# Projecting keys, queries and values for attention with 512 moving columns instead of 256

## The chip, the cores and the metric

The kernel runs on one core of one Trainium2 chip. The metric is the device time of one execution in microseconds (us), as the median of several runs. The profile and the trace are of one further execution. TensorE is PE in the profile (PEld: its weight loads), VectorE DVE, ScalarE ACT, GpSimd POOL, SyncE SP.

## The reference

512 tokens of 1024 channels go through two layers. Layer A is a state-space mixer with a gated feed-forward block; layer B is attention with a gated feed-forward block. What matters here is the attention of layer B: keys and values are projected from the normed stream, queries from the layer's own normed stream, keys and queries get an RMS norm per head, and the attention is stick-breaking.

```python
def shared_kv(h, kv_norm, w_kv, k_norm):
    k, v = jnp.split(rms_norm(h, kv_norm) @ w_kv, 2, axis=-1)
    k = rms_norm(k.reshape(bsz, seq, N_HEADS, HEAD_DIM), k_norm)
    v = v.reshape(bsz, seq, N_HEADS, HEAD_DIM)

def stick_breaking_attention(q, k, v):
    # A[t,s] = beta_ts * prod_{s<j<t}(1 - beta_tj), s < t
    z = jnp.einsum('bqhd,bkhd->bhqk', q, k) * HEAD_DIM ** -0.5
    log_beta = jax.nn.log_sigmoid(z)
    log_1m = jnp.where(causal, log_beta - z, 0.0)
    later = lax.cumsum(log_1m, axis=3, reverse=True) - log_1m
    w = jnp.where(causal, jnp.exp(log_beta + later), 0.0)
    return jnp.einsum('bhqk,bkhd->bqhd', w, v)

def sb_mixer(xn, w_q, q_norm, k, v, w_o):
    q = rms_norm((xn @ w_q).reshape(bsz, seq, N_HEADS, HEAD_DIM), q_norm)
    return stick_breaking_attention(q, k, v).reshape(bsz, seq, D_MODEL) @ w_o
```

There are 16 heads of 64 channels; all values are float32.

## The kernel before

Every large product is three matmuls: both operands are split into a rounded high half (fp32r) and the rest, and high by high, high by low and low by high are added in PSUM. `WStream` brings the weights in pieces: a DMA on SP loads a piece into one of three raw buffers (`_load`), ACT writes the high half (`high`, L116 or, with a gain, L119), DVE the low half (`low`, L130 or L133), each into one of `OUT` = 3 buffers. `take()` hands out the next piece and prepares `look` = 2 pieces ahead.

The attention stage runs from 601 to 862 us of the span. Its **main work** is the projection. `project(g)` for g = 0 to 3 takes four heads, and for each in turn keys, queries and values: 256 output columns over 4 token blocks and 8 blocks of channels. The token block of the stream is the stationary operand, the weight half the moving one, with 256 columns (L458 to L460). Two PSUM banks hold the four token blocks; after g = 0, which runs alone and uses banks 0 to 5, all projections use banks 0 and 1. Then values are copied out by ACT with the row scale (L465). Keys and queries are copied to `raw` (L470, two buffers), squared by ACT (L472), summed per head by DVE (L475), turned into a factor by some sixteen tiny DVE operations (L476 to L481, with `rsqrt` at L200 to L207), multiplied by it (L484, DVE), queries also by the gain row `grow` on POOL (L487), and split into a high half (L490, ACT) and a low half (L491, DVE): the tiles `ks` and `qs`, one buffer each.

The **side work** is the attention of the eight pairs of heads. `steps(pair)` does for each pair: transposes of `ks` and `qs` on PE (L517), copies of the result (L521; L525 to L527 for `kpad`), scores (`z`, L536, banks 2 to 4), two sigmoids on ACT (L558, L559), a scan and a product on DVE (L565, L566), transposes of the weights (L584, banks 5 and 7), a copy on ACT (L588), the product with values (L597, bank 6) and the copy of the output (L618, or straight into its halves). The scores of a pair lie in five units of up to 512 columns, so there are 40 units in the stage.

`schedule()` deals the side work out in small steps by the list `PAIR`. `attention()` issues one step of the projection after another and as many side steps as `MAIN_RATIO` allows; what is left of the side work goes between the matmuls of the output projection (`wo_part`, L250 to L252, by `WO_RATIO`), whose input is the pairs' outputs and whose result DVE adds to the stream (L657). After this a scheduler reorders each engine's instructions within what the buffers allow; the program's final order is therefore not the written one.

## Time and profile before

| | |
|---|---|
| median of 3 runs | 1239.07 us (1238.36 to 1240.52) |
| profiled execution, its own time | 1241.04 us |
| its span in the trace | 1239.3 us |
| PE busy in the span | 1199.9 us (97%) |
| DVE busy | 776.4 us (63%) |
| ACT busy | 542.9 us (44%) |
| POOL busy | 143.0 us (12%) |
| attention stage | about 601 to 862 us of the span |

The busy time of an engine is the sum of its instructions' times, where overlapping ones count once. Matmuls are pipelined: the duration of one (0.28 us with 256 columns) is longer than the distance from its start to the next one's start, and it is this distance that the time of a run of matmuls is made of. An engine's idle time costs something only where the others wait for it.

### The profile page before, as it was taken

The numbers are of one execution on the slowest core, as the hardware profiler recorded it, in microseconds if no ns is written. First come the engines' busy times: TensorE is split into PE (matmuls) and PEld (weight loads), VectorE is DVE, ScalarE is ACT, GpSimd is POOL, SyncE is SP. The second block draws the span as 40 slices with busy tenths as digits, with TensorE's granted clock in tenths as the row PEclk, the third lists the DMA queues.
The fourth block names the chain that finished last, engine by engine and source line by source line (L and its number), as shares of the span: only waits on it lengthen the run. The fifth ranks groups of instructions, "written<-read, shape, count | busy, mean of one in ns | idle before, by whom it ended". The sixth has DMA issues, their size and how long they took to land. (4 is left out here: it accounts for less than half of the span.)

```text
span 1239.3 us, 17202 instructions
## 1 busy us (share of the span) xinstructions
PE 1199.9 (97%) x6831; PEld 1012.5 (82%) x6831; DVE 776.4 (63%) x1246; ACT 542.9 (44%) x869; POOL 143.0 (12%) x132
## 2 busy tenths in 40 slices
PE   7888899999999999999999999999999999999998
PEld 7777777888888888888999898776788888888887
DVE  7969545867565564333579998976775556552322
ACT  7644543444333333222358676645453433332210
POOL 4878720000000000000000000000300000000000
PEclk8889999999999999999999999999999999999999
DMA  7333232333333333333321121121333333322330
GB/s 191 107 85 90 74 103 85 103 87 101 102 91 96 102 91 92 103 96 96 103 86 58 63 69 52 52 69 35 95 92 97 91 95 92 102 102 88 125 111 34
DMA packets 162379, 111.68 MB, mean 90 GB/s; under 512 B 7452, under 2 KB 151868, under 8 KB 162236
## 3 DMA queue, kind: packets, MB, share of 16 engines
q1 hardware_dynamic: 161724, 109.55, 29.9%
q8 instruction: 53, 0.87, 0.3%
q10 hardware_dynamic: 576, 1.05, 0.2%
q14 instruction: 26, 0.21, 0.1%
HBM read 101.93 MB, written 2.10 MB: 84 GB/s over the span
## 5 line engine op out<-in xcount | busy, mean ns | idle before, releaser
L250 PE MATMUL b<-t_xhi,t_whi 128*128 128x512 f32 x864 | 336.6, 392 | 2.6 <-ACT p_w L1340 1.4
L251 PE MATMUL b<-t_xlo,t_whi 128*128 128x512 f32 x864 | 337.3, 391 | 1.4 <-DVE t_xlo L168 0.8
L252 PE MATMUL b<-t_xhi,t_wlo 128*128 128x512 f32 x864 | 336.9, 390 | 0.2 <-DVE t_wlo L130 0.2
L116 ACT CAST t_whi<-t_wraw 128x1024 fp32r<-128x1024 f32 (+1 forms) x166 | 173.1, 1044 | 361.0 <-PE b L251 240.6
L130 DVE TENSOR_TENSOR t_wlo<-t_wraw,t_whi 128x1024 fp32r<-128x1024 f32 (+1 forms) x154 | 189.2, 1230 | 151.4 <-ACT t_whi L116 150.5
L250 PEld LDWEIGHTS b<-t_xhi,t_whi 128*128 128x128 f32 x864 | 162.4, 188 | 38.1 <-ACT p_w L1340 1.9
L251 PEld LDWEIGHTS b<-t_xlo,t_whi 128*128 128x128 f32 x864 | 162.4, 188 | 36.8 <-DVE t_xlo L168 2.7
L252 PEld LDWEIGHTS b<-t_xhi,t_wlo 128*128 128x128 f32 x864 | 162.3, 188 | 34.6 <-DVE t_wlo L130 0.6
L458 PE MATMUL b<-t_whi,t_xhi 128*128 128x256 f32 x384 | 109.3, 286 | 1.4 <-ACT a_raw L470 1.3
L460 PE MATMUL b<-t_whi,t_xlo 128*128 128x256 f32 x384 | 109.1, 285 | 0.0
L459 PE MATMUL b<-t_wlo,t_xhi 128*128 128x256 f32 x384 | 109.1, 285 | 0.0
L315 DVE TENSOR_TENSOR p_fg<-b,p_rsrow 128x512 f32<-128x512 f32 x44 | 30.4, 691 | 86.9 <-PE b L252 80.5
L458 PEld LDWEIGHTS b<-t_whi,t_xhi 128*128 128x128 f32 x384 | 73.2, 191 | 1.9 <-ACT a_raw L470 1.8
L326 DVE TENSOR_TENSOR p_fv<-b,p_rsrow 128x512 f32<-128x512 f32 x44 | 30.4, 690 | 69.5 <-PE b L252 69.5
L459 PEld LDWEIGHTS b<-t_wlo,t_xhi 128*128 128x128 f32 x384 | 73.4, 191 | 0.2
L460 PEld LDWEIGHTS b<-t_whi,t_xlo 128*128 128x128 f32 x384 | 73.2, 191 | 0.2
L250 PE MATMUL b<-p_ahi,t_whi 128*128 128x512 f32 x176 | 68.5, 389 | 0.0
L251 PE MATMUL b<-p_alo,t_whi 128*128 128x512 f32 x176 | 68.5, 389 | 0.0
L252 PE MATMUL b<-p_ahi,t_wlo 128*128 128x512 f32 x176 | 68.5, 389 | 0.0
L348 PE MATMUL b<-t_whi,p_ahi 128*128 128x512 f32 x176 | 68.5, 389 | 0.0
L349 PE MATMUL b<-t_wlo,p_ahi 128*128 128x512 f32 x176 | 68.5, 389 | 0.0
L350 PE MATMUL b<-t_whi,p_alo 128*128 128x512 f32 x176 | 68.5, 389 | 0.0
(307 smaller groups left out, 1892.9 us busy)
## 6 DMA issues: line engine op xcount, KB each, us to landing
t_wraw<-in_ffn_w_up_dram SPq DMA_DIRECT2D x88, 512.0 KB
t_wraw<-in_ffn_w_down_dram SPq DMA_DIRECT2D x30, 512.0 KB
t_wraw<-in_a_w_glu_dram SPq DMA_DIRECT2D x16, 512.0 KB
t_wraw<-in_w_kv_dram SPq DMA_DIRECT2D x16, 512.0 KB
t_wraw<-in_ffn_w_down_dram SPq DMA_DIRECT2D x16, 448.0 KB
t_wraw<-in_a_w_in_dram SPq DMA_DIRECT2D x8, 512.0 KB
p_w<-p_w2d SPq DMA_DIRECT2D x32, 128.0 KB
t_wraw<-in_b_w_q_dram SPq DMA_DIRECT2D x8, 512.0 KB
```

The lines of the kernel that those rows point to most:

```text
L116: nc.scalar.copy(hi, t)
L130: eng.tensor_tensor(out=lo, in0=t, in1=hi, op=ALU.subtract)
L250: nc.tensor.matmul(ps, whi, xhi, start=start, stop=False)
L251: nc.tensor.matmul(ps, whi, xlo, start=False, stop=False)
L252: nc.tensor.matmul(ps, wlo, xhi, start=False, stop=stop)
L315: nc.vector.tensor_tensor(out=g, in0=pg, in1=rr, op=ALU.mult)
L348: nc.tensor.matmul(pss[tb], xh, whi[:, j], start=k + j == 0, stop=False)
L349: nc.tensor.matmul(pss[tb], xh, wlo[:, j], start=False, stop=False)
L350: nc.tensor.matmul(pss[tb], xl, whi[:, j], start=False, stop=st)
L458: nc.tensor.matmul(reg[tb], xh, whi[:, j], start=st, stop=False, skip_group_check=True)
L459: nc.tensor.matmul(reg[tb], xh, wlo[:, j], start=False, stop=False, skip_group_check=True)
L460: nc.tensor.matmul(reg[tb], xl, whi[:, j], start=False, stop=k == 7, skip_group_check=True)
```

## The change

The projection is cut into six phases, `kq0, v0, kq1, kq2, v1, kq3`. A `kq` phase makes keys and queries of four heads, side by side as 512 columns; a `v` phase makes values of eight heads, also 512 columns. In a phase the four token blocks come one after the other, each with 24 matmuls of 512 columns (L501 to L503 now) into one bank, 0 and 1 in turn. All four pieces of the weights of a phase (two channel blocks by 512 columns each) have to be there for that, so there are five high and low buffers instead of three, two of them in the attention's pool (`half_tile`), and `AHEAD` prepares the next phase's pieces during the present one. A piece of a `kq` phase comes in two DMAs.

Keys and queries share one norm per phase: four norms with 32 factors instead of eight with 16. Each token block's bank is copied to `raw` by ACT (L509), squared in place in PSUM by ACT (L510) and summed by DVE out of PSUM (L511). `raw` has one buffer instead of two, the product with the factors is written back into it (L535), and `kh` is gone. The side work runs by `MAIN_RATIO` 0.85 after a delay of eight main steps; there are six instead of seven tiles for the attention weights. To make room, one row tile (`grow1`) moves from the constants into the pool of the first layer's setup, so that its load and the two POOL operations that use it come later.

```diff
     def _load(self, i):
         ap, nk, nc_, gain = self.plan[i][:4]
         t = self.e.tile([P, nk, nc_], F32, "wraw", self.RAW)
-        self.e.nc.sync.dma_start(t, ap.rearrange("(k p) c -> p k c", p=P))
+        for c, (a, _) in self.parts(i):
+            self.e.nc.sync.dma_start(t[:, :, c], a.rearrange("(k p) c -> p k c", p=P))
         self.raw[i] = t
+
+    def parts(self, i):
+
+        ap, nk, nc_, gain = self.plan[i][:4]
+        if not isinstance(ap, tuple):
+            return [(slice(0, nc_), (ap, gain))]
+        n = nc_ // len(ap)
+        return [(slice(j * n, (j + 1) * n), x) for j, x in enumerate(ap)]
+
+    def half_tile(self, i, tag):
+        shape = [P, *self.plan[i][1:3]]
+        if self.room is not None and (i - self.room[1]) % (self.OUT + 2) >= self.OUT:
+            return self.room[0](shape, F32R, tag, 2)
+        return self.e.tile(shape, F32R, tag, self.OUT)
 
...
-        hi = e.tile([P, nk, nc_], F32R, "whi", self.OUT)
+        hi = self.half_tile(i, "whi")
...
-                nc.scalar.activation(hi[:, k], t[:, k], AF.Copy, scale=gain[:, k : k + 1])
+                for c, (_, g) in self.parts(i):
+                    nc.scalar.activation(hi[:, k, c], t[:, k, c], AF.Copy, scale=g[:, k : k + 1])
...
+        self.prepare(i + self.look)
+        return self.done.pop(i)
+
+    def prepare(self, m):
...
-    acc = e.pt(pool, [P, T + LINE], F32, "ssacc")[:, :T]
+    acc = e.pt(pool, [P, T + 7 * LINE], F32, "ssacc")[:, :T]
...
+PHASES = (("kq", 0), ("v", 0), ("kq", 1), ("kq", 2), ("v", 1), ("kq", 3))
+
+AHEAD = {(2, 0): 1, (3, 1): 2, (3, 2): 3, (3, 3): 4}
+
+
 def attn_plan(w_kv, w_q, gkv, gb):
     plan = []
-    for g in range(4):
-        for w, c0, gain in ((w_kv, 0, gkv), (w_q, 0, gb), (w_kv, D, gkv)):
-            for k in (0, 4):
-                plan.append((w[k * P : (k + 4) * P, c0 + g * 256 : c0 + (g + 1) * 256], 4, 256, gain[:, k : k + 4]))
+    for kind, g in PHASES:
+        for k in range(0, DC, 2):
+            rows = slice(k * P, (k + 2) * P)
+            if kind == "v":
+                src = ((w_kv[rows, D + g * T : D + (g + 1) * T], gkv[:, k : k + 2]),)
+            else:
+                c = slice(g * 256, (g + 1) * 256)
+                src = ((w_kv[rows, c], gkv[:, k : k + 2]), (w_q[rows, c], gb[:, k : k + 2]))
+            plan.append((src, 2, T, True))
...
-MAIN_RATIO = 0.792
+MAIN_RATIO = 0.85
+
+DELAY = 8
...
-WB = 7
+WB = 6
...
-RB = 2
-KB = 1
...
+    def project(self, kind, g):
+        e, nc, ws = self.e, self.nc, self.ws
+        first = ws.i
+        tiles = []
+        if kind == "v":
+            out = self.t([P, 4, T], F32, "v", 2)
+        else:
+            out = self.t([P, 4, T], F32, "raw")
+            ms = self.t([P, 4, 8], F32, "hms")
+        for tb in range(4):
+            ps = e.bank(tb % 2)
+            for piece in range(4):
+                if tb == 0:
+                    tiles.append(ws.take())
+                elif (tb, piece) in AHEAD:
+                    ws.prepare(first + 4 + AHEAD[tb, piece])
+                whi, wlo = tiles[piece]
+                for j in range(2):
+                    k = 2 * piece + j
+                    xh = self.xhi[k][:, tb * P : (tb + 1) * P]
+                    xl = self.xlo[k][:, tb * P : (tb + 1) * P]
+                    nc.tensor.matmul(ps, xh, whi[:, j], start=k == 0, stop=False)
+                    nc.tensor.matmul(ps, xh, wlo[:, j], start=False, stop=False)
+                    nc.tensor.matmul(ps, xl, whi[:, j], start=False, stop=k == 7)
+                if piece < 3:
+                    yield
+            if kind == "v":
+                nc.scalar.activation(out[:, tb], ps, AF.Copy, scale=self.r4[:, tb : tb + 1])
+            else:
+                nc.scalar.copy(out[:, tb], ps)
+                nc.scalar.activation(ps, ps, AF.Square)
+                nc.vector.tensor_reduce(
+                    out=ms[:, tb], in_=ps.rearrange("p (h d) -> p h d", d=HD), axis=mybir.AxisListType.X, op=ALU.add)
+            if tb < 3:
+                yield
+        if kind == "v":
+            for i in range(2):
+                self.v[2 * g + i] = out[:, :, 256 * i : 256 * i + 256]
+        else:
+            self.norm(g, out, ms)
+        yield
+    def norm(self, g, raw, ms):
+        e, nc = self.e, self.nc
+        S = [P, 4, 8]
+        flat = lambda t: t.rearrange("p a b -> p (a b)")
+        nc.vector.tensor_tensor(out=ms, in0=ms, in1=self.r4sq.unsqueeze(2).broadcast_to(S), op=ALU.mult)
+        nc.vector.tensor_scalar(out=ms, in0=ms, scalar1=EPS, scalar2=None, op0=ALU.add)
+        f = self.t(S, F32, "hf")
+        rsqrt(e, flat(f), flat(ms), [P, 32], "hr")
+        nc.vector.tensor_tensor(out=f, in0=f, in1=self.r4.unsqueeze(2).broadcast_to(S), op=ALU.mult)
+        for i, kind in enumerate("kq"):
+            H = [P, 4, 4, HD]
+            kh = raw[:, :, 256 * i : 256 * i + 256].rearrange("p a (b c) -> p a b c", c=HD)
+            nc.vector.tensor_tensor(
+                out=kh, in0=kh, in1=f[:, :, 4 * i : 4 * i + 4].unsqueeze(3).broadcast_to(H), op=ALU.mult)
+            if kind == "q":
+                nc.gpsimd.tensor_tensor(
+                    out=kh, in0=kh, in1=self.grow.unsqueeze(1).unsqueeze(1).broadcast_to(H), op=ALU.mult)
+            ks = self.t([P, 16, 2, HD], F32R, f"{kind}s", SB)
+            hi, lo = (ks[:, :, j].rearrange("p (a b) c -> p a b c", a=4) for j in range(2))
+            nc.scalar.copy(hi, kh)
+            nc.vector.tensor_tensor(out=lo, in0=kh, in1=hi, op=ALU.subtract)
+            self.st[g, kind] = ks
...
-        for _ in a.project(0):
+        ws.room = a.t, ws.i
+        for _ in a.project(*PHASES[0]):
             pass
         side = a.schedule()
-        n = main = 0
-        for g in range(1, 4):
-            for _ in a.project(g):
+        n, main = 0, -DELAY
+        for phase in PHASES[1:]:
+            for _ in a.project(*phase):
                 main += 1
                 while n < main * MAIN_RATIO:
                     next(side, None)
                     n += 1
+        ws.room = None
...
-        self.gr = [e.tile([P, HD], F32, f"grow{i}") for i in range(2)]
+        self.gr = [e.tile([P, HD], F32, "grow0")]
...
-            gr = self.gr
+            gr = self.gr + [e.pt(pool, [P, HD], F32, "grow1")]
             nc.sync.dma_start(gr[0], a["k_norm"].partition_broadcast(P))
             nc.sync.dma_start(gr[1], a["b_q_norm"][0].partition_broadcast(P))
             nc.gpsimd.tensor_tensor(out=gr[0], in0=gr[0], in1=gr[1], op=ALU.mult)
```

Three places show how the order of the instructions moves. The names are those of the buffers: `b_0_5390` is a use of PSUM bank 0, the last number tells uses apart; `t_xhi_5223` to `5230` are the eight channel blocks of the stream; `a_ks`, `a_qs`, `a_raw`, `a_w` are the tiles named above.

**First place**, PE, where the first block of the projection ends and a bank is used again. Before, keys of the first four heads end in bank 1, and queries go on in banks 2 and 3:

```order
L458 MATMUL b_1_5285<-t_whi,t_xhi_5227 128x256
L459 MATMUL b_1_5285<-t_wlo,t_xhi_5227 128x256
L460 MATMUL b_1_5285<-t_whi,t_xlo_5235 128x256
L458 MATMUL b_2_5437<-t_whi,t_xhi_5220 128x256
L459 MATMUL b_2_5437<-t_wlo,t_xhi_5220 128x256
L460 MATMUL b_2_5437<-t_whi,t_xlo_5228 128x256
```

Now token blocks 0 and 1 of `kq0` alternate and end within three matmuls of each other, and token block 2 goes into bank 0 at once:

```order
L501 MATMUL b_0_5289<-a_whi,t_xhi_5230 128x512
L501 MATMUL b_1_5362<-a_whi,t_xhi_5230 128x512
L502 MATMUL b_0_5289<-a_wlo,t_xhi_5230 128x512
L503 MATMUL b_0_5289<-a_whi,t_xlo_5238 128x512
L502 MATMUL b_1_5362<-a_wlo,t_xhi_5230 128x512
L503 MATMUL b_1_5362<-a_whi,t_xlo_5238 128x512
L501 MATMUL b_0_5390<-t_whi,t_xhi_5223 128x512
L502 MATMUL b_0_5390<-t_wlo,t_xhi_5223 128x512
```

The use of a free bank between two uses of bank 0 is gone here.

**Second place**, where the transposes of a new `ks` stand. PE before (third pair; `b_0` and `b_1` are banks of a projection that is under way):

```order
L459 MATMUL b_1_6632<-t_wlo,t_xhi_5226 128x256
L517 MATMUL b_5_6705<-p_identr,a_ks 128x128 x4
L597 MATMUL b_6_6449<-a_wt,a_v 64x512 x2
L517 MATMUL b_7_6713<-p_identr,a_ks 128x128 x4
L460 MATMUL b_1_6632<-t_whi,t_xlo_5234 128x256
L458 MATMUL b_0_6631<-t_whi,t_xhi_5227 128x256
```

PE now (third pair; `b_1_6137` is token block 1 of `kq2`, `b_0_6199` its token block 2):

```order
L503 MATMUL b_1_6137<-t_whi,t_xlo_5238 128x512
L648 MATMUL b_6_5838<-a_wt,a_v 64x512 x2
L568 MATMUL b_7_6059<-p_identr,a_ks 128x128 x4
L568 MATMUL b_5_6067<-p_identr,a_ks 128x128 x4
L635 MATMUL b_7_6075<-t_ident,a_w 128x128 x4
L501 MATMUL b_0_6199<-t_whi,t_xhi_5223 128x512
```

and DVE now at the same place (the norm of `kq1` ends with L535; `b_0_6084` is token block 0 of `kq2`, in the bank that `b_0_6199` wants):

```order
L535 TENSOR_TENSOR a_raw<-a_raw,a_hf 128x4x256 x2
L543 TENSOR_TENSOR a_ks<-a_raw,a_ks 128x16x64
L617 TENSOR_TENSOR a_w<-a_w,a_cp_5283 128x128
L617 TENSOR_TENSOR a_w<-a_w,a_cp_5283 128x384
L616 SCALAR_TENSOR_TENSOR a_cp_5281<-a_cp_5281,p_edge 128x256 x2
L617 TENSOR_TENSOR a_w<-a_w,a_cp_5281 128x256 x2
L669 COPY a_o_5959<-b_6_5838 128x512
L576 CAST a_kpad_5265<-b_7_6059 128x512
L543 TENSOR_TENSOR a_qs<-a_raw,a_qs 128x16x64
L576 CAST a_kpad_5267<-b_5_6067 128x512
L578 CAST a_kpad_5266<-b_7_6059 64x512
L511 TENSOR_REDUCE a_hms<-b_0_6084 128x8
```

Before, main matmuls that waited for nothing stood around the transposes; now the transposes of `ks` and a bank that has to be emptied stand one behind the other on PE.

**Third place**, PE behind the last matmul of the projections. Before, the first transposes of `ks` behind it are those of the seventh pair:

```order
L252 MATMUL b_0_7783<-t_xhi_7769,t_wlo 128x512
L517 MATMUL b_7_7738<-p_identr,a_ks 128x128 x4
L250 MATMUL b_0_7783<-t_xhi_7773,t_whi 128x512
L251 MATMUL b_0_7783<-t_xlo_7774,t_whi 128x512
L252 MATMUL b_0_7783<-t_xhi_7773,t_wlo 128x512
L597 MATMUL b_6_7492<-a_wt,a_v 64x512 x2
L517 MATMUL b_5_7746<-p_identr,a_ks 128x128 x4
```

Now they are those of the sixth:

```order
L587 MATMUL b_2_6817<-a_kpad_5267,a_fmq 128x256
L587 MATMUL b_2_6817<-a_kpad_5268,a_fmq 128x256
L568 MATMUL b_5_6829<-p_identr,a_ks 128x128 x4
L648 MATMUL b_6_6627<-a_wt,a_v 64x512 x2
L568 MATMUL b_7_6837<-p_identr,a_ks 128x128 x4
L273 MATMUL b_0_7074<-t_xhi_7070,a_whi 128x512
```

In all, 11 of the 40 units of scores stood behind the last projection matmul on PE, and 20 stand there now. Up to the last product with values, PE changed 129 times between projection or output-projection matmuls and side work, and changes 89 times now.

## Rows read from the trace of the kernel before

**Rows 1.** Windows: span, busy of PE, PEld, DVE, ACT, POOL, granted clock, DMA share, GB/s.

```profile
601.00:640.00 39.00, 39.00 (x326) 38.92 (x325) 27.58 (x82) 19.60 (x41) 4.54 (x14) 1.00 0.27 89
640.00:792.00 152.00, 150.40 (x1204) 137.97 (x1203) 138.25 (x297) 107.20 (x206) 7.78 (x4) 1.00 0.20 63
792.00:862.00 70.00, 65.12 (x348) 47.33 (x347) 51.87 (x81) 35.33 (x61) 0.00 (x0) 1.00 0.18 53
```

**Rows 2.** Timeline of PE, projection without side work: start, duration, instruction; 26 steps apart.

```profile
613.76 0.28 PE L458 MATMUL b<-t_whi,t_xhi 128*128 128x256 f32 x1
...
616.88 0.28 PE L460 MATMUL b<-t_whi,t_xlo 128*128 128x256 f32 x1
```

**Rows 3.** Timeline of PE, 512 columns in the feed-forward block; 15 steps apart.

```profile
1149.78 0.39 PE L348 MATMUL b<-t_whi,p_ahi 128*128 128x512 f32 x1
...
1153.18 0.39 PE L348 MATMUL b<-t_whi,p_ahi 128*128 128x512 f32 x1
```

**Rows 4.** Timeline of PE, side work between projection matmuls.

```profile
681.41 0.63 PE L536 MATMUL b<-a_kpad,a_fmq 128*128 128x256 f32 x4
681.98 1.08 PE L597 MATMUL b<-a_wt,a_v 128*64 128x384 f32 x8
683.00 0.66 PE L584 MATMUL b<-t_ident,a_w 128*128 128x128 f32 x4
...
683.78 0.35 PE L458 MATMUL b<-t_whi,t_xhi 128*128 128x256 f32 x1
683.97 0.28 PE L459 MATMUL b<-t_wlo,t_xhi 128*128 128x256 f32 x1
```

**Rows 5.** Timeline of PE at a wait; in brackets idle time and what ended it.

```profile
771.79 0.28 PE L460 MATMUL b<-t_whi,t_xlo 128*128 128x256 f32 x1
773.42 0.39 PE L458 MATMUL b<-t_whi,t_xhi 128*128 128x256 f32 x1 [1.35 <-ACT a_raw L470]
```

**Rows 6.** Lines by shape, 595 to 870 us: count, busy us, mean ns, idle before.

```profile
L133 DVE SCALAR_TENSOR_TENSOR t_wlo<-t_wraw,t_va,t_whi 128x256 fp32r<-128x256 f32 x92 | 44.0, 523 | 10.8 <-ACT t_whi L119 10.7
L484 DVE TENSOR_TENSOR a_kh<-a_raw,a_hf 128x1024 f32<-128x1024 f32 x8 | 9.8, 1222 | 0.2
L475 DVE TENSOR_REDUCE a_hms<-a_kh 128x16 f32<-128x1024 f32 x8 | 9.8, 1219 | 3.0 <-ACT a_kh L472 3.0
L470 ACT COPY a_raw<-b 128x512 f32<-128x512 f32 x16 | 9.1, 588 | 8.1 <-PE b L460 7.6
```

**Rows 7.** Timeline of DVE, side work and tiny norm operations mixed.

```profile
656.38 0.15 DVE L476 TENSOR_TENSOR a_hms<-a_hms,a_r4sq 128x16 f32<-128x16 f32 x1
656.44 1.22 DVE L565 TENSOR_TENSOR_SCAN a_cp<-a_cp,p_edge 128x512 f32<-128x512 f32 x1
657.58 0.73 DVE L566 TENSOR_TENSOR a_w<-a_w,a_cp 128x128 f32<-128x128 f32 x2
...
659.14 0.69 DVE L525 CAST a_kpad<-b 128x512 fp32r<-128x512 f32 x1
659.75 0.68 DVE L566 TENSOR_TENSOR a_w<-a_w,a_cp 128x512 f32<-128x512 f32 x1
660.35 1.22 DVE L565 TENSOR_TENSOR_SCAN a_cp<-a_cp,p_edge 128x512 f32<-128x512 f32 x1
```

**Rows 8.** Timeline of DVE, tiny norm operations one behind the other.

```profile
671.10 0.18 DVE L204 TENSOR_TENSOR t_hrt<-t_hri 128x16 f32<-128x16 f32 x1
671.31 0.18 DVE L205 SCALAR_TENSOR_TENSOR t_hrt<-t_hrt,a_hms 128x16 f32<-128x16 f32 x1
```

**Rows 9.** Timeline of DVE while POOL multiplies (the POOL row, then the DVE rows).

```profile
694.43 2.40 POOL L487 TENSOR_TENSOR a_kh<-a_kh,t_grow 128x1024 f32<-128x1024 f32 x1 [54.04 <-ACT t_whi L119]
...
695.01 3.29 DVE L133 SCALAR_TENSOR_TENSOR t_wlo<-t_wraw,t_va,t_whi 128x256 fp32r<-128x256 f32 x4
```

**Rows 10.** Timeline of POOL at the start of the program.

```profile
24.60 0.41 POOL L1492 TENSOR_SCALAR t_grow<-t_grow 128x64 f32<-128x64 f32 x1
34.11 2.80 POOL L130 TENSOR_TENSOR t_wlo<-t_wraw,t_whi 128x1024 fp32r<-128x1024 f32 x1 [9.10 <-ACT t_whi L116]
```

More of the change, by code (lines that the diff above doesn't have):

```diff
@@ L91, in __init__ @@
         self.look = self.OUT - 1
+        self.room = None
     def _load(self, i):
@@ L127, in low @@
         t, hi = self.half.pop(i)
-        lo = e.tile([P, nk, nc_], F32R, "wlo", self.OUT)
+        lo = self.half_tile(i, "wlo")
         if gain is None:
@@ L132, in low @@
             for k in range(nk):
-                nc.vector.scalar_tensor_tensor(
-                    out=lo[:, k], in0=t[:, k], scalar=gain[:, k : k + 1], in1=hi[:, k],
-                    op0=ALU.mult, op1=ALU.subtract)
+                for c, (_, g) in self.parts(i):
+                    nc.vector.scalar_tensor_tensor(
+                        out=lo[:, k, c], in0=t[:, k, c], scalar=g[:, k : k + 1], in1=hi[:, k, c],
+                        op0=ALU.mult, op1=ALU.subtract)
         self.done[i] = (hi, lo)
@@ L141, in take @@
         self.i += 1
+        self.prepare(i + self.look)
+        return self.done.pop(i)
+    def prepare(self, m):
         n = len(self.plan)
-        while self.ld < min(n, i + self.look + self.RAW - 1):
+        while self.ld < min(n, m + self.RAW - 1):
             if self.ld - self.sp >= self.RAW:
@@ L146, in take @@
             self.ahead(self.ld + 1)
-        self.split(min(n, i + self.look))
-        return self.done.pop(i)
+        self.split(min(n, m))
 def split_x(e, srcs, gain, tag="x"):
@@ L424, in __init__ @@
         self.st = {}
-        self.r4sq = self.t([P, 4], F32, "r4sq")
+        self.r4sq = self.t([P, 4 + LINE], F32, "r4sq")[:, :4]
         e.nc.vector.tensor_tensor(out=self.r4sq, in0=r4, in1=r4, op=ALU.mult)
@@ L442, in t @@
         return lined(self.pool.tile, shape, dt, name=f"a{self.e.n}_{tag}", tag=tag, bufs=bufs)
-    def project(self, g):
+    def project(self, kind, g):
         e, nc, ws = self.e, self.nc, self.ws
-        for i, kind in enumerate(("k", "q", "v")):
-            b0 = 2 * i if g == 0 else 0
-            pss = [e.bank(b0), e.bank(b0 + 1)]
-            reg = [pss[tb // 2][:, (tb % 2) * 256 : (tb % 2) * 256 + 256] for tb in range(4)]
-            for piece in range(2):
-                whi, wlo = ws.take()
-                for j in range(4):
-                    k = 4 * piece + j
-                    for tb in range(4):
-                        xh = self.xhi[k][:, tb * P : (tb + 1) * P]
-                        xl = self.xlo[k][:, tb * P : (tb + 1) * P]
-                        st = k == 0 and tb % 2 == 0
-                        nc.tensor.matmul(reg[tb], xh, whi[:, j], start=st, stop=False, skip_group_check=True)
-                        nc.tensor.matmul(reg[tb], xh, wlo[:, j], start=False, stop=False, skip_group_check=True)
-                        nc.tensor.matmul(reg[tb], xl, whi[:, j], start=False, stop=k == 7, skip_group_check=True)
+        first = ws.i
[21 more added lines that the diff above has]
+                if piece < 3:
@@ L493, in project @@
-            yield
+                nc.scalar.activation(out[:, tb], ps, AF.Copy, scale=self.r4[:, tb : tb + 1])
+            else:
+                nc.scalar.copy(out[:, tb], ps)
[9 more added lines that the diff above has]
+            self.norm(g, out, ms)
```

29 lines of the change are left out of this document (removed).

## The prediction

> **What bounds the kernel now.** I read the windows by stage first, then the timeline of PE, then the groups by shape, and last the timelines of DVE and POOL at the places that the new order makes tight. In the windows [rows 1] the reader is to see that PE is the bound of the attention stage: it is busy 39.00 of 39.00 us while the first projection runs alone, 150.40 of 152.00 while projections and side work alternate, and 65.12 of 70.00 in the tail, where the output projection takes the projections' place. The granted clock is 1.00 in all three, so nothing in the change can win clock there. DVE is the second engine: 138.25 of 152.00 (91%) in the middle, 51.87 of 70.00 (74%) in the tail. DMA is at 0.18 to 0.27. So PE's own work is what the change can shorten, and DVE is the engine that can take it back. About 0.2% (2.5 us) is what a measurement of this kernel can tell from no change.
>
> The sum is made against the profiled execution, 1241.04 us (span 1239.3), which lies 2.0 us above the median of 1239.07; I carry the difference over to the median.
>
> **Matmuls: -7.7 us.** 1152 matmuls of 256 columns become 576 of 512. With 256 columns, 26 steps from start to start take 3.12 us [rows 2]: 0.120 each, 138.2 us. With 512 columns of the same operand type, 15 steps take 3.40 us [rows 3]: 0.2267 each, 130.6 us. The Trainium skill ("TensorE: Matmul & The Clock Gate", section "Back-to-back issue gap") gives a warm distance of N/2.4 + 2.5 ns, 109 and 216 ns: as an estimate from that page the gain would be only 1.5 us and the sum 6.2 us worse. The trace's 120 and 227 ns decide.
>
> **Changes between main and side work: -2.8 us.** After a piece of side work the first projection matmul is 0.19 us from the next [rows 4], not 0.12: 0.07 lost. Four score matmuls of 256 columns before it took 0.57 (681.41 to 681.98) where 0.48 would do: the way out costs a like amount. There are 40 changes fewer: -2.8; if only the way back counts, -1.4.
>
> **The wait for L470: -1.5 us.** At 771.79 PE stands until 773.42 for a copy out of the bank it needs [rows 5], 1.63 less the usual 0.12. Place and order are gone after the change.
>
> Side work on PE and everything outside the stage is unchanged in count and order, so a microsecond of PE here is a microsecond of the end. That makes -12.0. What comes back:
>
> **First place, bank 0 in `kq0`: +1.8.** Blocks 0 and 1 end together and block 2 wants bank 0 at once. The bank must be copied (0.59, L470 [rows 6]), squared and summed. A square of 512 columns in place in PSUM has no row; ACT's copy of 512 out of PSUM, 0.59, is the nearest. The sum over 512 columns is half of L475's 1.22 [rows 6]. 1.8 in all, less the two block 1 matmuls that still run (0.45), plus three handovers. There is no side work yet to fill it. I take 1.8; the ends are 1.3 and 2.2.
>
> **Second place, `kq1` to `kq2`: +5.** `raw` has one buffer, so the copy of `kq2`'s block 0 waits until the low half of `kq1`'s queries is made, and block 2 waits for that bank. Count DVE from the end of `kq1`'s last matmul: copy, square and sum 1.8; four scans of 512 columns at 1.14 (656.44 to 657.58), three products and two low halves at about 0.6, as 659.75 to 660.35 [rows 7]; 16 tiny operations at between 0.06, where other work stands behind (656.38 to 656.44 [rows 7]), and 0.21 one behind the other [rows 8]; two L535 of 1.2, as L484 [rows 6]. That is 13 to 15.4 us, say 13.7. Then L543 of the keys, 1.2. POOL's product for the queries, 2.40, starts with it, and in [rows 9] four L133 that began on DVE beside such a product took 3.29 us, where four make 2.1 by their mean of 0.523 [rows 6]. So `ks` is there at about 17, or 16 if POOL does not hold it. The Trainium skill ("SBUF — State Buffer", section "Who interferes with whom") says that a DVE instruction with two SBUF inputs and a GpSimd one that reads SBUF share a port pair as an exclusive lock; the 3.29 us agree. Without such a hold the term would be about 1 lower.
>
> PE has until there 48 matmuls (10.9 us), scores, products and transposes of about 5.9 by [rows 4] and 0.5 for changes: it arrives at 17 too, and the transposes wait little. But behind them on PE stands the first matmul of block 2, and DVE does before the sum of block 0: products, two scans of 256, a copy, three `kpad` copies at 0.6 to 0.7, L543 of the queries 1.2 and the sum 0.6, in all 6.7 us, against 1.2 of transposes on PE. So 4.5 to 5.5 of wait; I take 5, with ends 3 (tiny operations cheap, POOL holds nothing) and 7 (all at 0.21, full hold). The other phases are parted by a `v` phase or lie before the side work, and `raw` is free in time.
>
> **Third place, the tail: +4.** Nine units of scores more, 20 instead of 11, stand behind the last projection matmul, because the projections now end earlier and give the side work less room. A unit is a scan, a product and a share of `kpad` on DVE: 1.14 + 0.60 + 0.5 [rows 7], 2.2, so 20 us, and some 3 of `kq3`'s norm. On PE the unit's scores, transposes and product with values are some 1.5 [rows 4]: 13 us. DVE, 51.87 of 70.00 us before [rows 1], comes to about 75 of 83 (90%). Low end 0: in the middle stage DVE was at 91% and PE lost only 1.6 of 152 us [rows 1]. High end 10: there the projection filled in; here the output projection itself needs the pairs' outputs, and the 10 us by which PE's work exceeded DVE's (65.12 against 51.87 less the waits) are used up, so that each unit's wait shows. Between them I take 4, nearer the low end, since rows of the middle stage show the same load.
>
> **Small edits.** `grow1`: its load and two POOL operations of at most 0.41 move behind the idle stretch that ends at 34.11 (9.10 us, [rows 10]) into POOL's busy one: 0 to 0.8, taken as 0.4. The joint norm halves the tiny DVE operations; what DVE gains is in the sums above. The low halves have as many columns as before. The 40 weight loads for 24 move the same bytes at a DMA share of 0.27 or less [rows 1], and splits are issued phases ahead: nothing, unless DVE falls behind by more than a phase; then PE would wait for `wlo`. Six tiles instead of seven for the weights: nothing while the transposes keep pace; its price is part of the tail's high end. Values in 8 copies instead of 16: ACT is at 107.20 of 152.00, nothing.
>
> **Sum.** -7.7 - 2.8 - 1.5 + 1.8 + 5 + 4 + 0.4 = -0.8: 1240.2 for the profiled execution, **1238.3 us** against the median. With all unknowns at their low ends -7.7 (1231.4), at the high ones +9.4 (1248.5).
>
> **Rivals.** *Faster: DVE hides.* The tail behaves like the middle stage, PE waits no more than before: 1238.3 - 4 = 1234.3; with the second place at 3 as well, 1232. For it speaks DVE at 91% beside a full PE [rows 1], and that the norm gives DVE back half its tiny operations; against it the 20 units in a row with nothing else on PE than the output projection.
>
> *Slower: DVE becomes the bound of the tail.* The nine units moved behind the projections, with `kq3`'s norm among them and POOL's product holding DVE once more, make DVE's work there longer than PE's. It decides as soon as DVE's sum from the last projection matmul to the last output's low half passes PE's; by my sums the two are about equal (75 and 78), where before they were 52 and 65. Price 10 instead of 4: 1238.3 + 6 = 1244.3.
>
> *Slower: no gain per column.* Should 512 columns cost what twice 256 do in this place (weight loads and matmuls spaced by columns alone), the -7.7 falls away: 1246.0. Against it stands every row of the feed-forward block with 512 columns [rows 3]. The Trainium skill's page on TensorE, named above, points this way, with 1.5 of the 7.7 left.
>
> That the change does not do what it says I give no chance: the new order holds 576 matmuls of 512 columns.
>
> **How the numbers follow.** The forecast, gain and waits cancelling, within 0.2%: 0.36, own range 1236.5 to 1241.5. Tail hidden, 1234.3: 0.21; tail and second place, 1232: 0.15. DVE bound in the tail, 1244.3: 0.25. No gain per column, 1246: 0.03. Faster 0.36, same 0.36, slower 0.28. Signs are open, so the range must reach both rivals; 1231 to 1246 leaves out about 2 in 10.
>
> **What would show it.** In the changed profile: projection matmuls 0.227 us apart; a gap of about 2 us on PE after the first 48, ended by a DVE sum; a gap of 4 to 6 before `kq2`'s block 2, with ScalarE's copy into `raw` late behind L543 of the queries; in the tail gaps on PE ended by L616 or L617, some 4 us more in sum than the 4.88 of before. No gap at `kq2` makes the second place wrong; a tail with PE idle no longer than before gives the first rival; a tail with DVE above 95% and PE idle over 12 us the second.

## The result

The changed kernel takes 1251.82 us (median of 4 runs, 1250.34 to 1252.52) against 1239.8 for the kernel before: a ratio of 1.0096, 95% interval 1.0084 to 1.0108. It is slower by about 12 us, where no change was forecast and the range ended at 1246.

Where the 11.4 us between the two profiled spans lie can be read at fixed places of PE's timeline. The first projection matmul starts at 602.68 us (601.37 before), the feed-forward block of layer B at 880.18 (869.79), the last matmul at 1244.91 (1234.55), the end is at 1250.7 (1239.3). So 9.1 us are in the attention stage, nothing between it and the last matmul, 1.3 ahead of it and 1.0 behind the last matmul. Neither of the two is shown to be an effect of the change: in the fifteen profiles of kernels with the changed first layer the stage begins anywhere from 595.1 to 602.7 us, in the four with that of before from 599.7 to 601.9, and from the feed-forward block of layer B to the end all nineteen take 368.8 to 370.5 us. (The sections above end the stage at 862 us; some matmuls of the output projection run from there to 869.79.)

The windows of the whole stage and of its two parts, projections and tail (columns as in [rows 1]), before:

```profile
601.37:869.79 268.42, 261.79 (x1905) 229.86 (x1903) 223.81 (x467) 167.28 (x317) 14.96 (x19) 1.00 0.20 62
...
601.37:791.78 190.41, 188.81 (x1525) 176.38 (x1524) 165.61 (x377) 126.70 (x247) 12.32 (x17) 1.00 0.21 68
791.78:869.79 78.01, 72.97 (x383) 53.48 (x381) 58.19 (x91) 40.59 (x71) 2.64 (x2) 1.00 0.16 48
```

and after:

```profile
602.68:880.18 277.50, 259.70 (x1328) 201.51 (x1327) 210.44 (x395) 163.23 (x301) 16.54 (x19) 0.98 0.19 60
...
602.68:778.70 176.02, 168.01 (x840) 134.83 (x839) 129.80 (x260) 106.70 (x202) 11.52 (x16) 0.98 0.22 70
778.70:880.18 101.48, 91.69 (x489) 66.68 (x488) 80.63 (x136) 56.53 (x100) 5.02 (x3) 0.97 0.14 42
```

PE is idle for 17.8 us of the stage (277.50 - 259.70), where it was for 6.6: 8.0 instead of 1.6 in the projections, 9.8 instead of 5.0 in the tail. And the granted clock is no longer 1.00. In windows of 4 us, I multiply PE's busy time by the share of the clock that was not granted; the sum, an estimate of what the slow stretches cost, is 4.8 us. What is left, 255.0 us of PE's work at full clock, is 6.8 less than the 261.8 before. So the stage's +9.1 is **-6.8 of work, +11.2 of idle time, +4.8 of clock.** DVE is busy 13 us less than before (210.44 for 223.81): it has not become the bound by its amount of work.

The waits of PE in the stage:

```profile
PE b L635 <- DVE a_kpad L578: 6.2, 2, 5.8
PE b L273 <- ACT t_xhi L187: 4.4, 3, 2.4
PE b L635 <- DVE a_w L617: 1.7, 1, 1.7
PE b L501 <- DVE a_hms L511: 1.5, 1, 1.5
PE b L274 <- DVE t_xlo L188: 1.2, 1, 1.2
```

The longest, on PE's timeline, with what follows it:

```profile
695.96 0.88 PE L568 MATMUL b<-p_identr,a_ks 128*128 128x128 f32 x8
702.66 1.11 PE L635 MATMUL b<-t_ident,a_w 128*128 128x128 f32 x4 [5.81 <-DVE a_kpad L578]
703.42 0.78 PE L501 MATMUL b<-t_whi,t_xhi 128*128 128x512 f32 x1
...
704.42 0.63 PE L503 MATMUL b<-t_whi,t_xlo 128*128 128x512 f32 x1
704.85 0.63 PE L501 MATMUL b<-t_whi,t_xhi 128*128 128x512 f32 x1
```

This is the second place of the prediction, the third pair's `ks`. Behind the wait the matmuls are 0.43 us apart, not 0.227, because the clock has fallen:

```profile
696.00:700.00 4.00, 0.84 (x10) 0.70 (x8) 4.00 (x8) 1.05 (x1) 0.50 (x1) 0.92 0.00 0
700.00:704.00 4.00, 1.34 (x6) 1.24 (x7) 3.84 (x6) 3.24 (x6) 0.00 (x0) 0.50 0.00 0
704.00:708.00 4.00, 4.00 (x14) 3.20 (x13) 0.80 (x2) 0.58 (x1) 0.00 (x0) 0.72 0.01 4
```

In the first two rows PE idles while DVE is full. DVE's timeline there; in between stands POOL's product, and on the last row ACT's copy of `kq2`'s block 0 into `raw`:

```profile
690.72 2.33 DVE L535 TENSOR_TENSOR a_raw<-a_raw,a_hf 128x1024 f32<-128x1024 f32 x2
693.03 1.22 DVE L543 TENSOR_TENSOR a_ks<-a_raw,a_ks 128x1024 fp32r<-128x1024 f32 x1
...
693.22 3.27 POOL L538 TENSOR_TENSOR a_raw<-a_raw,t_grow 128x1024 f32<-128x1024 f32 x1 [52.35 <-DVE a_raw L535]
...
694.17 2.94 DVE L617 TENSOR_TENSOR a_w<-a_w,a_cp 128x128 f32<-128x128 f32 x2
...
700.08 1.21 DVE L543 TENSOR_TENSOR a_qs<-a_raw,a_qs 128x1024 fp32r<-128x1024 f32 x1
701.21 0.68 DVE L576 CAST a_kpad<-b 128x512 fp32r<-128x512 f32 x1
701.92 0.69 DVE L578 CAST a_kpad<-b 64x512 fp32r<-64x512 f32 x1
702.63 1.48 DVE L511 TENSOR_REDUCE a_hms<-b 128x8 f32<-128x512 f32 x2
...
701.32 0.58 ACT L509 COPY a_raw<-b 128x512 f32<-128x512 f32 x1 [0.55 <-DVE a_qs L543]
```

The two products at 694.17 (128 columns, which the row names, and 384) take 2.94 us beside POOL's product; two such took 0.73 without one [rows 7].

Two holds end here almost together. The transposes L635 wait for the `kpad` copy, which ends at 702.6. The first matmul of block 2, next on PE at 703.42, needs bank 0: since `raw` has one buffer, ACT copies that bank only when DVE has made the low half of the queries (700.08 and 1.21), and the sum out of the bank, the first of the two L511, ends at about 703.4. Without the first hold PE would still have stood until 703.4 for the second.

The keys come later too. The low half of the second group's keys starts 75.5 us behind the first projection matmul in the kernel before (676.85 us) and 90.4 us behind it now (693.03), and the side work that needs them starts later with them:

```profile
676.85 1.22 DVE L491 TENSOR_TENSOR a_ks<-a_kh,a_ks 128x1024 fp32r<-128x1024 f32 x1
```

### The profile page after: what moved, and what is told of

It is laid out like the page before. It is cut to its first block, busy times and chain, and to the rows that moved or that the text cites. A ratio compares the mean times of both kernels' runs of the same rounds, so it can differ in the third digit from the quotient of the medians.

```text
span 1250.7 us, 16000 instructions
## 1 busy us (share of the span) xinstructions
PE 1200.0 (96%) x6255; PEld 986.0 (79%) x6255; DVE 765.0 (61%) x1174; ACT 538.1 (43%) x853; POOL 143.9 (12%) x132
## 5 line engine op out<-in xcount | busy, mean ns | idle before, releaser
L345 ACT ACTIVATE p_fc<-p_fc 128x512 f32<-128x512 f32 x44 | 27.7, 632 | 75.6 <-DVE p_fc L342 75.5
L616 DVE TENSOR_TENSOR_SCAN a_cp<-a_cp,p_edge 128x128 f32<-128x128 f32 (+2 forms) x64 | 49.6, 811 | 9.2 <-ACT a_cp L609 9.2
L501 PE MATMUL b<-t_whi,t_xhi 128*128 128x512 f32 x120 | 48.1, 400 | 1.5 <-DVE a_hms L511 1.5
L503 PE MATMUL b<-t_whi,t_xlo 128*128 128x512 f32 x120 | 47.5, 397 | 0.0
L502 PE MATMUL b<-t_wlo,t_xhi 128*128 128x512 f32 x120 | 47.3, 396 | 0.0
```

What stands on the lines that cost most here:

```text
L501: nc.tensor.matmul(ps, xh, whi[:, j], start=k == 0, stop=False)
L502: nc.tensor.matmul(ps, xh, wlo[:, j], start=False, stop=False)
L503: nc.tensor.matmul(ps, xl, whi[:, j], start=False, stop=k == 7)
L616: nc.vector.tensor_tensor_scan(rev, rev, c["edge"][:, T - n :][:, ::-1], 0.0, ALU.mult, ALU.add)
```

## The experiments

In each, "stage" is the time from the first projection matmul to the feed-forward block in the profiled run, "idle" is the stage less PE's busy time in it, "clock loss" is the estimate described above, and the ratio is to the kernel before, measured beside it. A stage is read from one profile; the two kernels whose stage was taken twice gave 277.5 and 278.3 us (the changed one) and 268.4 both times (the kernel before, the second time with only `grow1` moved). The changed kernel once more:

> The changed kernel once more, with a second profile. Theory (its attention stage is 9.1 us longer, and the 1.3 us before it and 1.0 us behind it in the first pair of profiles differ from run to run): the stage again takes 276.5 to 278.5 us, the time before the stage lies anywhere between 595 and 603 us, and the median is 9 to 11 us above the kernel before. Rival (the change also lengthens the first layer): first projection matmul at 602 us or later again, 12 us or more above.

Stage 278.3 us from 595.4 on, idle 17.3, clock loss 6.3; median 1248.6 (6 runs), ratio 1.0073 (1.0059 to 1.0087). The stage repeats, its start does not; the median is 9.1 us above the kernel before, as much as the stage's part in the first pair of profiles.

**grow1 alone**, in the kernel before:

```diff
-        self.gr = [e.tile([P, HD], F32, f"grow{i}") for i in range(2)]
+        self.gr = [e.tile([P, HD], F32, "grow0")]
...
-            gr = self.gr
+            gr = self.gr + [e.pt(pool, [P, HD], F32, "grow1")]
```

> The kernel before with one part of the change alone: grow1 lies in the pool of the first layer's setup, so its load and the two POOL operations come later. Theory (the 1.3 us by which the attention stage starts later in the changed kernel, 602.7 instead of 601.4 us, come from this move): 1241.1 us, first projection matmul at 602.7. Rival (they come from the rest of the change, or differ from run to run): 1239.8, first projection matmul at 601.4.

1239.53 us, ratio 0.999 (0.9978 to 1.0001), first projection matmul at 597.2, stage 268.4 us. The move costs nothing that these runs can tell, as the rival had it.

**Three parts of the second place.** The product with the gain row left out; the queries' product with the factors (`fr`) written to two of the six weight tiles, with POOL's product and both halves of `qs` in two parts each; a third bank for the projection, which leaves two for the scores:

```diff
-            if kind == "q":
-                nc.gpsimd.tensor_tensor(
-                    out=kh, in0=kh, in1=self.grow.unsqueeze(1).unsqueeze(1).broadcast_to(H), op=ALU.mult)
```

```diff
...
+                for b in range(2):
+                    s = slice(2 * b, 2 * b + 2)
+                    o = self.t([P, T], F32, "w", WB).rearrange("p (a b c) -> p a b c", a=2, c=HD)
+                    nc.vector.tensor_tensor(out=o, in0=kh[:, s], in1=fr[:, s], op=ALU.mult)
...
```

```diff
-ZB = 3
+ZB = 2
...
-            ps = e.bank(tb % 2)
+            ps = e.bank((0, 1, 4)[self.mb % 3])
+            self.mb += 1
```

> The changed kernel without POOL's product of the queries with the gain row (the gain is left out of the queries). Theory (the product holds DVE, and this makes most of the 5.8 us wait of L635 behind the third pair's ks transposes): the wait falls to about 3, the granted clock stays at 1.00 behind it, and with the like in the tail 1246 us. Rival (the wait is the sum of DVE's own work in its queue): the wait falls by 1 to 2 us only, the clock drops all the same, 1250 us.

1244.05 us, ratio 1.0034 (1.0021 to 1.0047); stage 274.5, idle 13.6. The wait behind the `ks` transposes is 2.1 us, and now it is block 2's first matmul that waits for the sum out of bank 0. The clock fell all the same, to 0.76 and 0.81 in the next two windows. Without POOL's product more than half of the wait is gone; that the clock would hold was wrong.

> The changed kernel, where the queries' product with the factors goes into two of the six weight tiles instead of back into raw, so that raw is free as soon as the norm has read it. Theory (the wait is for the kpad copies in DVE's queue, not for raw): the wait at the third pair's ks transposes stays above 4 us, 1250 to 1252 us. Rival, as the prediction had it (the single raw buffer holds up bank 0): the wait falls below 2 us, 1246 us.

1253.19 us, ratio 1.0115 (1.0092 to 1.0138); stage 281.3, idle 19.1, clock loss 7.2. The wait breaks into 1.4 ahead of the transposes and 2.1 behind, 3.6 in all instead of 5.8, but the tail idles 13.4 us instead of 9.8. This doesn't tell what a free `raw` is worth: the keys still lie in it, ACT's copy of `kq2`'s block 0 starts at 689.92 where the low half of the keys ends (688.68 and 1.21), and the attention has two weight tiles less meanwhile.

> The changed kernel with three banks in turn for the projection (0, 1, 4) and two instead of three for the scores, so that on PE a whole token block of kq2 stands before the third pair's ks transposes. Theory (the losses are waits of PE for DVE with nothing else to do, and each costs clock besides): the wait there falls from 5.8 to under 1.5 us, the granted clock stays at 1.00 there, and the time falls by 6 to 8 us, to about 1245; the tail's waits stay. Rival (DVE's work bounds the whole stage, so that filling in only moves the wait): the wait comes back within 30 us, 1250 us or more.

1242.66 us, ratio 1.002 (1.0006 to 1.0033); stage 271.3, idle 12.4, clock loss 3.5. That is 9.2 us below the changed kernel's first median and 5.9 below its second. A whole token block now stands ahead of the transposes, and the place reads

```profile
692.85 0.80 PE L570 MATMUL b<-p_identr,a_ks 128*128 128x128 f32 x8
694.75 0.50 PE L503 MATMUL b<-t_whi,t_xhi 128*128 128x512 f32 x1 [1.10 <-DVE a_hms L513]
695.09 0.40 PE L504 MATMUL b<-t_wlo,t_xhi 128*128 128x512 f32 x1
```

with the matmuls 0.23 us apart behind it. The keys are no earlier (their low half 93.4 us from the first projection matmul, 90.4 in the changed kernel): PE just has something else to do, and what is left of the wait is still one for a bank's sum. The wait did not come back in the projections; the tail kept its own and idles 11.0 us.

**The gain product on DVE** (`nc.gpsimd.tensor_tensor` becomes `nc.vector.tensor_tensor`), in the changed kernel, with three banks, and in the kernel before:

> The changed kernel with the queries' product with the gain row on DVE instead of POOL: DVE has 1.2 us more work in each of four norms, but is not held for 2.4 to 2.9. Theory that the hold makes the second place's wait: the wait falls from 5.8 to about 4 us, the time by 2 to 4 us, 1248 to 1250. Rival (the queue's own length decides): no change or 1 to 2 us slower, 1252 to 1254.

1246.71 us, ratio 1.0056 (1.0042 to 1.0071); stage 275.2, the wait 4.8 instead of 5.8: the way of the theory, with 1.0 us where it had 1.8. The ratio is lower than the changed kernel's first, 1.0096, but not clearly lower than its second, 1.0073 (to 1.0087).

> The changed kernel with three banks in turn for the projection (two for the scores) and the gain product on DVE: the two edits that each made it faster. Theory (they take different waits away: the one at the second place, and POOL's hold in the tail): stage 268 to 270 us, 1240 us, level with the kernel before. Rival (they take the same wait away): no better than three banks alone, 1242 to 1243.

1241.71 us, ratio 1.0018 (1.0007 to 1.0029); stage 272.5. It is no better than three banks alone, as the rival had it.

> The kernel before with the queries' gain product on DVE instead of POOL. Theory (in the kernel before the hold was covered): no change within 2 us, 1238 to 1241. Rival (the hold costs a microsecond or two wherever it falls): 1237 or less.

1235.55 us, ratio 0.9971 (0.9959 to 0.9982): **faster than both kernels.** Stage 266.1, idle 3.9, and one wait of 1.9 us, with 1.7 of clock behind it; the tail idles 1.8 us instead of 5.0. The rival, that the hold was not covered in the kernel before either, fits. That the hold alone is what cost there is not shown, since the order of the instructions moves with the edit too.

> The kernel before with the gain product on DVE and three banks in turn for the projection behind the first group (two for the scores). Theory (the one long wait left in the middle stage, 2.0 us of PE for a product with values behind a full bank pair, and the clock loss of 1.7 behind it go): stage 262 to 264 us, 1232 to 1234. Rival (two score banks cost as much as the third bank gives): 1235 or more.

1240.0 us, ratio 1.0 (0.9992 to 1.0009); stage 268.1. The wait went, another of 3.1 us came in the tail, as the rival had it.

**The phases.** Values of four heads, with 256 columns, behind each `kq` phase; the plan of the weights and the pace of the side work (`MAIN_RATIO` 0.905, `DELAY` 1) change with them:

```diff
-PHASES = (("kq", 0), ("v", 0), ("kq", 1), ("kq", 2), ("v", 1), ("kq", 3))
+PHASES = (("kq", 0), ("v", 0), ("kq", 1), ("v", 1), ("kq", 2), ("v", 2), ("kq", 3), ("v", 3))
```

> The changed kernel with values in phases of four heads (256 columns) behind each kq phase instead of eight heads in two phases: kq0, v0, kq1, v1, kq2, v2, kq3, v3, side work by 0.905 after one step. 384 of the 576 matmuls keep 512 columns. Theory (the wide v0 phase ahead of kq1 and the phase kq3 at the very end bring keys and queries late, so that the side work starves, runs 12 to 20 us late and falls into the tail, where PE waits for it and loses clock): the third pair's ks transposes come 82 to 86 us after the first projection matmul (82.0 before, 93.3 in the changed kernel), PE's idle time in the stage falls from 17.7 to 8 us or less, the clock loss to under 1 us, the stage takes 265 to 267 us instead of 277.5, and the kernel 1237 us. Rival (the joint norm and POOL's product in DVE's queue make the waits, whatever the phases): a wait of over 3 us stays behind the third pair's ks transposes and the tail keeps its two waits, 1246 us or more.

1241.79 us, ratio 1.0021 (1.0011 to 1.0031); stage 270.8, idle 10.4, clock loss 1.4. The loss shrank, but not as I had it, and less: `kq1` ends at 63.5 instead of 74.4 us, and the third pair's transposes still stand at 91.9. The keys come no earlier; the value phase behind `kq1` gives PE work meanwhile, as the third bank does, and no wait of a microsecond stands there.

> As the kernel with values in phases of four heads, and raw with two buffers, three banks in turn for the projection and two for the scores. Theory of the late side work: the same or up to 2 us faster, 1235 to 1237 us, since little waiting is left to fill. Rival (bank 0 and raw hold PE up): 4 us or more faster than with two banks and one raw buffer.

1245.31 us, ratio 1.005 (1.0034 to 1.0066); stage 273.3. Neither expectation holds: it is slower, with a new wait of 2.8 us for the copy of a value bank at 178 us.

> The changed kernel with values in phases of four heads and the gain product on DVE. Theory (the two losses add up, and most of the 512-column gain for keys and queries shows): stage 266 to 268 us, 1237 to 1239, at or just under the kernel before, above its version with the gain product on DVE. Rival (the joint norm's latency alone keeps it behind): stage 270 us or more, 1241 or more.

1245.76 us, ratio 1.0045 (1.003 to 1.006); stage 275.0, with a wait of 5 us at 67 us ahead of the transposes of `qs`. The stage is the rival's, though this wait is not the norm's. The edits do not add: each moves the scheduler's order, and PE meets its waits elsewhere.

**The norm's way.** The tiny operations on POOL, all but one (the same formula, `nc.gpsimd` for `nc.vector`, four instructions for three in a step):

> The changed kernel with the tiny norm operations (32 columns) on POOL instead of DVE, where scans and products stood between them: from the last sum to L535 13.7 us in the changed kernel at the end of kq1. Theory (the norm's way through DVE's queue brings ks late, and so the side work): the low half of the second group's keys is made 5 us earlier than 90.4 us from the first projection matmul or more, the stage is 3 to 6 us shorter, 1246 us. Rival (POOL's own time and its hold on DVE eat it up): no change, 1250 to 1253.

1258.17 us, ratio 1.0145 (1.0124 to 1.0166); stage 287.2. They take 0.24 to 0.52 us each on POOL, and the keys come at 94.4. With three banks and the gain product on DVE:

> As the one before, and the tiny norm operations on POOL. Theory of the late keys: another 2 to 4 us off, 1237 us, faster than the kernel before. Rival: no change, 1240 to 1242.

1249.72 us, ratio 1.0082 (1.0065 to 1.0098); stage 277.7: slower by 8 us than without it. The theory that the norm's way through DVE's queue is what costs falls in this form.

**DVE's amount of work.** The products of the scans left out:

```diff
-                nc.vector.tensor_tensor(out=b[:, o : o + n], in0=b[:, o : o + n], in1=s, op=ALU.mult)
```

> The changed kernel without the products of L617 (40 scan results are not multiplied in): some 20 us less work for DVE, nothing less for PE. Theory (DVE is the second bound, and the waits are its backlog): PE's idle time falls from 17.5 to under 10 us, the clock loss to under 2, the stage to 262 to 266 us, and against the kernel before without the same products it is 2 to 5 us shorter. Rival (the waits are latencies of the joint norm, the POOL product and the bank chain): the stage stays above 270 us and above the kernel before's.

> The kernel before without the products of L566. Theory (DVE's backlog cost the kernel before little, since the projections filled in): the stage falls from 268.4 to 264 to 267 us only, pure work stays at 261.8. Rival: it falls as much as the changed kernel's does, by 10 us or more.

Changed: 1242.54 us (ratio 1.0016, 1.0005 to 1.0026), stage 270.7, idle 12.7, clock loss 3.4. Before: 1229.83 us (ratio 0.9917, 0.9902 to 0.9932), stage 259.0, idle 0.2, no clock loss. The windows of the stage, changed kernel first:

```profile
598.90:869.55 270.65, 257.92 (x1329) 200.38 (x1327) 187.09 (x331) 163.72 (x301) 15.85 (x19) 0.98 0.19 62
```

```profile
599.73:858.76 259.03, 258.84 (x1904) 229.71 (x1903) 197.24 (x403) 166.88 (x317) 16.45 (x19) 1.00 0.21 64
```

The theory that DVE's amount is the second bound falls for the changed kernel: with DVE busy 187 of 271 us PE still idles 12.7, and the distance to the kernel before grows from 9.1 to 11.6 us. DVE's amount has a part in it all the same: the stage is some 7 us shorter than with the products. In the kernel before it holds: 27 us less DVE work let all of its idle time go, and the stage fell by 9.4 us, more than the theory there allowed (4.4) and just short of the rival's 10. PE's busy time fell by 3.0 us with it (261.79 to 258.84), though it has the same instructions: so busy time is not pure work, and some of it goes with the order of the instructions or is waiting too short to show as idle. What the changed kernel waits for is, for the most part, a chain. Its DVE timeline without the products, from the end of `kq1`:

```profile
678.36 0.68 DVE L511 TENSOR_REDUCE a_hms<-b 128x8 f32<-128x512 f32 x1
...
685.56 0.19 DVE L531 TENSOR_TENSOR a_hf<-a_hf,t_rstd 128x32 f32<-128x32 f32 x1
685.78 2.36 DVE L535 TENSOR_TENSOR a_raw<-a_raw,a_hf 128x1024 f32<-128x1024 f32 x2
688.06 3.43 DVE L616 TENSOR_TENSOR_SCAN a_cp<-a_cp,p_edge 128x256 f32<-128x256 f32 x2
691.41 1.19 DVE L543 TENSOR_TENSOR a_ks<-a_raw,a_ks 128x1024 fp32r<-128x1024 f32 x1
```

Between the last sum and the keys lie 13 us even so. The tiny operations take 6 of them from the first to the last, with a low half of the weights and three scans among them, and POOL's hold of two scans takes 2.2 (3.43, where two such take 1.26 at 697.04 in the changed kernel).

**The tail.** The output projection's first part cut in two, in the changed kernel with three banks:

```diff
-WO_PARTS = ((0, 4), (4, 6), (6, 8))
+WO_PARTS = ((0, 2), (2, 4), (4, 6), (6, 8))
```

> The changed kernel with three banks in turn for the projection, and the output projection's first part of four pairs cut into two of two pairs (8 more additions on DVE, 5 us). Theory (behind the projections PE waits for the fourth pair's output, and has matmuls to do if the first pairs suffice): the two waits of 3.3 and 2.3 us at 180 us from the first projection matmul go, with the clock loss behind them, stage 266 to 268 instead of 271.3 to 272.5. Rival (DVE is behind, whatever PE does): the waits come back at the transposes, stage 271 or more.

1246.57 us, ratio 1.0057 (1.0038 to 1.0076); stage 276.5. The waits at 180 us went and came back at 213 and 218 us as 2.4 and 3.0, as the rival had it. PE can do the first pairs' part earlier; that the outputs of the later pairs are late whatever stands first is what I conclude, and it is not shown apart.

## Why the prediction was wrong

The mechanism of the waits in the projections and their places were right, the forecast was not: of the three terms that make the +9.1, the waits came near, the gain was sized too high, and the clock had no price at all.

- **Matmuls, -7.7: nearly right.** In the changed kernel 30 steps take 6.81 us (619.29 to 626.10 on PE's timeline), 0.227 each, as [rows 3] had it. 576 of them make 130.8 us against 138.2.
- **Changes between main and side work, -2.8: wrong.** Work at full clock fell by 6.8 us in all, not 10.5. Half of the term was misread: of the 0.57 us from the first score matmul to the product with values [rows 4], 0.21 is the step from the last score to the product (681.77 to 681.98), which no change of work makes, and the step from the projection to the scores (681.30 to 681.41) is the usual one. The 0.07 us behind a piece of side work [rows 4] did not turn into a gain with fewer changes, as far as the busy time can tell, which is not pure work.
- **The wait for L470, -1.5: right.** It is gone.
- **First place, +1.8:** 1.49 us of idle at `kq0`'s third block, ended by the DVE sum, as described; 0.71 more for a low half of the weights, which I had put at nothing.
- **Second place, +5:** 5.81 us. The low half of the keys ended at 694.25, about 17 us behind `kq1`'s last matmul (677.12), as forecast. PE stopped one row ahead of the bank, at L635, whose bank 7 waits for a `kpad` copy. The chain described ended 0.8 us later: ACT's copy into `raw` waited for L543 of the queries, and block 2 stood behind the sum of block 0. In the runs without POOL's product and with three banks the wait that is left is one for a bank's sum. No run gave `raw` a second buffer alone, so its price stays open. By its own terms the way to L543 sums to 12.7 to 15.1, not 13 to 15.4; nothing hangs on it. The rule of the Trainium skill ("SBUF — State Buffer", section "Who interferes with whom"), as the prediction has it, agrees with the 2.94 us.
- **Tail, +4:** idle rose from 5.0 to 9.8 us, so the size came out right, by luck. The sign that it named was hardly there: of the gaps over 1 us one, 1.75 us, was ended by L617, and the others by the high and low halves of the pairs' outputs (2.44 and 1.80 for L187, 1.19 for L188). Its reason, DVE as the near bound, was only argued then, and the changed kernel without the products speaks against it: 7.5 of the 9.8 us stay. The "10 us by which PE's work exceeded DVE's" are 13.3 by the rows, or 8.4 less the waits.
- **grow1, +0.4:** 0.
- **The clock: the step that failed.** "The granted clock is 1.00 in all three, so nothing in the change can win clock there" looked only at what could be won, and the sum put what could be lost at nothing. The wait of 5.81 at the second place and two places in the tail, one with a wait of 2.44 and one with 1.80 and 1.75, each left PE at the lower level for some microseconds: by the estimate 4.8 us in the first profile, 6.3 in the second. From the sum of -0.8 the stage's +9.1 is reached by 3.7 of gain that did not come (6.8 for 10.5), 4.8 of clock, 1.9 of idle time (11.2 for 9.3), less 0.4 for grow1. The range had the clock in neither of its ends. That the high end of the sum, +9.4, meets the stage's +9.1 is chance: it had 10 for the tail's waits and nothing for the clock.

My second rival had the direction, but not the mechanism: by its own sign DVE would be above 95% busy in the tail and PE idle for over 12 us, and DVE was busy 80.63 of 101.48 us (79%), PE idle for 9.8. What stays open: which link of the chain from the last projection matmul of a `kq` phase to the third pair's transposes would have to go. Shorter DVE work, the tiny operations on POOL and an earlier `kq1` each left the keys at 89 to 94 us. The wait behind them shrank without POOL's product, and went where independent matmuls stood ahead of it. A second buffer of `raw` alone and a joint norm split into keys and queries were not tried, and what makes the tail's waits was not found.

## What to carry to other kernels

Price a wait of PE twice: its own length, and the slow stretch that can follow (5.8 us and, by the three windows above, some 1.9 at the second place). When a change makes the bound engine's work shorter and coarser, ask what independent work stands in its queue at each hand-over to the others; two smaller phases that overlap the other's norm may be worth more than fewer, wider matmuls; no run here tried that. And an operation put on a free engine to relieve another is only a relief if it does not hold it: here POOL's product stretched two scans from 1.26 to 3.43 us, and with that product on DVE itself the old kernel was 0.3% faster.

## What the hardware showed unexpectedly

Waits that did and did not cost clock: a wait of 5.81 us behind eight transposes was followed by windows of 0.50 and 0.72, and one of 1.9 us behind projection matmuls, in the kernel before with the gain on DVE, by a window of 0.60; 1.49 us inside the first projection, and 1.10 behind eight transposes with three banks, by 1.00. The length alone does not tell: in the run with values in phases of four heads and the gain on DVE, a wait of 1.53 us behind projection matmuls was followed by 0.60. A clock of 0.50 is the 1.2 GHz level; before each fall PE had been at 1.00, the 2.4 GHz level.

In these traces POOL's tensor product holds a DVE operation of two SBUF operands until it ends: of the two products at 694.17 the first ends at 696.65, and POOL's ends at 696.50. And it grows itself when it starts beside one: 3.27 us, begun 0.2 us after L543, against 2.40 [rows 9].
